# Finishing a decoder layer's output rows beside the longest of 32 experts, run last

## The chip, the cores and the metric

One Trainium2 chip, one of its cores. The metric is device time in microseconds (us) of one launch of the whole layer, the median of several runs.

## What is computed

A decoder layer on 1024 tokens of 1024 features, in f32: a mixer (dilated attention beside a gated linear recurrence), then a mixture of experts. Only the second half matters here:

```python
x = x + gate_m * rms_norm(mixer(...), g_post_mix)          # called x1 below
h = modulate(rms_norm(x, g_pre_ffn), shift_f, scale_f)
top_val, top_idx = lax.top_k(h @ w_router + b_router, 4)   # 4 of 32 experts for each token
gates = softmax(top_val)
# for each chosen expert e of a token:
hg = h @ w_gu[e] + b_gu[e]                                  # 1024 x 2048
act = min(glu, 7) * sigmoid(1.702 * min(glu, 7)) * (clip(lin, -7, 7) + 1)
y += gate * (act @ w_down[e] + b_down[e])                   # 1024 x 1024
x = x + gate_f * rms_norm(y, g_post_ffn)                    # the output
```

An output row needs its token's whole sum y, since the norm is over the row.

## The kernel before, in words

The mixer ends with `mix_out_tile` (L1367), eight times for 128 tokens: it makes x1, stores it straight into the output tensor (L1405, queue of SyncE, SP), stores the rows h of the experts in `hrows` (L1416), and routes. `y_init` (L225) writes to `yacc`, a tensor in HBM, what the down biases give each token; the experts add to it. The experts are sorted by their number of tokens, and rank k gets `CAPS[k]` columns (L26): 352, 288, 256, ... 136 for ranks 0 to 15 (class `Many`), 128 for ranks 16 to 29 (`Few`), 64 for ranks 30 and 31 (`Half`). Tokens beyond the capacity go to a loop at the end, `overflow` (L1503), which has nothing to do on these inputs.

`moe` (L661) runs the ranks in the order `ORDER` (L28): 1, 30, 0, 31, then 2, 16, 3, 17, ... 15, 29. An expert's weights come in 12 pieces of 1 MB, eight for `gu` (the first product and the gating) and four for `down`. SP loads a piece into one of four raw buffers (L307, L313); ScalarE (ACT) copies it to a rounded high part `wh`, and VectorE (DVE) makes the rest `wl` (`split`, L268), four instructions of each. TensorE (PE) multiplies three times, high by high, low by high and high by low. In `Many` the weights stand still and the tokens move (`gemm`, L514), 48 matmuls of n columns' work a piece; with n of 192 to 256, `down` has the tokens stand still and 512 columns of weights move (`down_rows`, L349), 12 matmuls for each block of 128 tokens and piece; larger and smaller `Many` turn the product by PE transposes (L585). `Few` take 12 matmuls of 512 columns a piece, `Half` 8. The product is scaled by the gate on its way out of PSUM, and POOL (GpSimd) adds the rows to `yacc` with an indirect accumulating DMA (`scatter`, L624), one expert's after the other's. The next expert's first quarter of `gu` stands between the current one's `gu` and `down`. `Side` (L635) holds work cut into steps, transposes above all, and after each piece runs up to two steps of what is due; the tile framework then orders the instructions of each engine by priority in the order they were written, and each engine runs its own in order. POOL's queue is in order too: an expert's table and gathers stand behind the last one's additions.

Behind the last expert comes `overflow`, then `final_load` (L1421: the post-norm weights times gate_f, and the loading of the Sqrt table) and `final` (L1432): eight tiles of `yacc` loaded by SP, squared with a row sum on ScalarE, a scale factor from five small VectorE operations and a Sqrt, one product, and an accumulating store on POOL's queue, which adds the tile to x1 in the output (L1456).

Of the kernel before, what the change touches and what calls it, by code (L numbers as in the profile page):

```python
# [27 lines left out]
ORDER = [1, 30, 0, 31] + [k for i in range(2, 16) for k in (i, 14 + i)]  # L28
# [64 lines left out]
def moe_setup(g, tc, cst, wk, dram):  # L93
# [3 lines left out]
    g.yacc = dram.tile([T + TRASH, D], F32, name="yacc")  # L97
    z = wk.tile([128, D], F32, name="zrow", tag="pj")
    nc.vector.memset(z, 0.0)
    nc.gpsimd.dma_start(g.hrows[T:T + TRASH, :], z)  # L100
    nc.gpsimd.dma_start(g.yacc[T:T + TRASH, :], z)
    n = E * TROW // 128
# [15 lines left out]
    g.scats, g.x1st = [], []  # L118
# [366 lines left out]
class Many(Expert):  # L485
# [45 lines left out]
    def gu(self, c, side):  # L531
# [20 lines left out]
        nc.scalar.activation(sg, gl[:, :, 0], AF.Sigmoid, scale=1.702)  # L552
# [40 lines left out]

def get_table(b):
# [5 lines left out]
    b.tab = g.cst.tile([128, 3, 2], I32, name="tab", bufs=3)  # L600
# [60 lines left out]
def moe(g, tc, wp, wk, sm, ps):  # L661
    g.pieces, g.gathered = 0, None
    todo = [(Many if CAPS[k] > 128 else Few if CAPS[k] > 64 else Half)(g, tc, k, (wp, wk, sm, ps)) for k in ORDER]
# [8 lines left out]
    for nxt in todo[1:] + [None]:  # L672
        if nxt:
            prep = nxt.prep()
            side.add(prep)
        side.add(cur.gu(1, side))
# [12 lines left out]
    side.until(last)  # L689
    g.last_y = cur.y[0]  # L690
# [21 lines left out]
def rstd_sqrt(nc, sm, out, ssq, n, shape, name, bufs=None):  # L712

    kw = {} if bufs is None else {"bufs": bufs}
    v = sm.tile(shape, F32, name=name, **kw)
    z = sm.tile(shape, F32, name=name + "z", **kw)
# [7 lines left out]
    return root  # L724

# [637 lines left out]
def mix_out_tile(g, tc, t, wk, sm, ps):  # L1363
# [31 lines left out]
    for hf, cs in enumerate(halves):  # L1395
# [8 lines left out]
        nc.scalar.activation(hT[:, 4 * hf:4 * hf + 4, :].rearrange("p a b -> p (a b)"), pt, AF.Copy)  # L1404
    g.x1st.append(nc.sync.dma_start(g.out[0, tsl, :], x).ins)  # L1405
# [15 lines left out]
def final_load(g, tc, wk, sm):  # L1421
    nc = tc.nc
    g.gf = wk.tile([128, D], F32, name="gf", tag="gl")
    t0 = wk.tile([128, D], F32, name="gf2", tag="gl")
    nc.sync.dma_start(g.gf, g.g_post_ffn.to_broadcast([128, D]))
    nc.sync.dma_start(t0, g.mod_d[5:6, :].to_broadcast([128, D]))
    nc.vector.tensor_mul(g.gf, g.gf, t0)
    one = sm.tile([128, 1], F32, name="f_one")
    nc.scalar.activation(one, g.last_y[:, 0:1], AF.Sqrt, scale=0.0)


def final(g, tc, wp, wk, sm):  # L1432

    nc = tc.nc
    for t in range(0, NT, 2):
        ys = []
        sq = sm.tile([128, 2], F32, name="f_sq", bufs=2)
        for a in range(2):
# [132 lines left out]
def layer(ctx: ExitStack, tc: tile.TileContext, args):  # L1571
# [49 lines left out]
    sm = ctx.enter_context(tc.tile_pool(name="sm2", bufs=1))  # L1621
    moe(g, tc, wp, wk, sm, ps)
    overflow(g, tc, wp, wk, sm, ps)
    final_load(g, tc, wk, sm)
    final(g, tc, wp, wk, sm)


# [20 lines left out]
```

## Time and profile before

| | us |
|---|---|
| three runs: median (lowest to highest) | 2341.78 (2330.75 to 2345.35) |
| the profiled execution: time | 2336.89 |
| its span, first to last instruction | 2335.3 |
| PE busy | 2204.5 (94%) |
| VectorE busy | 1754.9 (75%) |
| ScalarE busy | 1439.3 (62%) |
| POOL busy | 287.5 (12%) |

The profile is of one execution. Busy PE time is a sum over pipelined matmuls whose ends are modelled, so it isn't work at peak rate. An engine counts as idle while it issues DMAs or waits. A number such as L1456 is the line of the kernel before.

### The profile page before, as it was taken

The numbers are of one execution on the slowest core, as the hardware profiler recorded it, in microseconds if no ns is written. First come the engines' busy times: TensorE is split into PE (matmuls) and PEld (weight loads), VectorE is DVE, ScalarE is ACT, GpSimd is POOL, SyncE is SP. The second block draws the span as 40 slices with busy tenths as digits, with TensorE's granted clock in tenths as the row PEclk, the third lists the DMA queues.
The fourth block names the chain that finished last, engine by engine and source line by source line (L and its number), as shares of the span: only waits on it lengthen the run. The fifth ranks groups of instructions, "written<-read, shape, count | busy, mean of one in ns | idle before, by whom it ended". The sixth has DMA issues, their size and how long they took to land. (4 is left out here: it accounts for less than half of the span.)

```text
span 2335.3 us, 38804 instructions
## 1 busy us (share of the span) xinstructions
PE 2204.5 (94%) x13342; PEld 1869.2 (80%) x13342; DVE 1754.9 (75%) x3881; ACT 1439.3 (62%) x3094; POOL 287.5 (12%) x244
## 2 busy tenths in 40 slices
PE   6999999998986999999999999999999999999991
PEld 3766667886766999888788888979999899889881
DVE  6466547556775675878787787978889899889883
ACT  6343442333445674876676676767777777777772
POOL 1000000000233020201110111101201111111101
PEclk9999999998987999999999999999999999999995
DMA  7333201113337695989888898989999999999996
GB/s 264 109 100 106 77 19 51 37 46 115 127 136 239 222 281 180 291 261 300 255 287 276 270 304 261 319 263 304 313 285 320 311 293 317 307 303 322 312 298 154
DMA packets 399217, 527.62 MB, mean 226 GB/s; under 512 B 17204, under 2 KB 308332, under 8 KB 397928
## 3 DMA queue, kind: packets, MB, share of 16 engines
q1 hardware_dynamic: 381296, 471.93, 61.1%
q0 software_dynamic: 16384, 48.54, 9.1%
q10 hardware_dynamic: 1336, 4.63, 0.5%
q8 instruction: 106, 1.74, 0.3%
q14 instruction: 95, 0.78, 0.1%
HBM read 485.29 MB, written 39.75 MB: 225 GB/s over the span
## 5 line engine op out<-in xcount | busy, mean ns | idle before, releaser
L281 DVE TENSOR_TENSOR wl<-raw,wh 128x512 fp32r<-128x512 f32 x1536 | 974.0, 683 | 149.7 <-ACT wh L280 59.5
L280 ACT ACTIVATE wh<-raw 128x512 fp32r<-128x512 f32 x1536 | 852.5, 624 | 242.9 <-DMA raw<-in_w_down_dram 65.6
L528 PE MATMUL pgb<-xb,wh 128*128 128x288 f32 (+13 forms) x2304 | 472.7, 332 | 4.4 <-DVE gl L548 3.9
L528 PEld LDWEIGHTS pgb<-xb,wh 128*128 128x128 f32 x2304 | 360.2, 190 | 13.3 <-DVE gl L548 4.9
L528 PE MATMUL pgb<-xb,wl 128*128 128x288 f32 (+15 forms) x2048 | 301.1, 274 | 0.0
L528 PEld LDWEIGHTS pgb<-xb,wl 128*128 128x128 f32 x2048 | 290.3, 190 | 5.3 <-DVE wl L281 0.2
L625 POOL DMA_INDIRECT yacc<-y,tab x52 | 114.7, 2206 | 1031.7 <-ACT y L369 488.9
L288 PE MATMUL pg<-wh,xh 128*128 128x512 f32 x448 | 180.8, 404 | 0.0
L289 PE MATMUL pg<-wh,xl 128*128 128x512 f32 x448 | 175.8, 392 | 0.0
L528 PE MATMUL pdb<-ab,wh 128*128 128x288 f32 (+7 forms) x768 | 142.5, 314 | 0.0
L988 PE MATMUL pp<-hh,pwh 128*128 128x512 f32 x448 | 130.4, 411 | 8.0 <-DVE y L1048 4.4
L546 ACT ACTIVATE gl<-pgb,bcol 128x288 f32<-128x288 f32 (+15 forms) x256 | 94.1, 421 | 70.8 <-PE pgb L528 70.5
L988 PE MATMUL pp<-hl,pwh 128*128 128x512 f32 x448 | 130.6, 408 | 0.8 <-DVE hl L925 0.8
L988 PE MATMUL pp<-hh,pwl 128*128 128x512 f32 x448 | 129.1, 406 | 0.0
L291 PE MATMUL pg<-wl,xh 128*128 128x512 f32 x448 | 120.8, 392 | 0.0
L528 PEld LDWEIGHTS pdb<-ab,wh 128*128 128x128 f32 x768 | 115.1, 189 | 1.0
L988 PEld LDWEIGHTS pp<-hh,pwh 128*128 128x128 f32 x448 | 82.3, 193 | 26.4 <-DVE y L1048 4.8
L291 PEld LDWEIGHTS pg<-wl,xh 128*128 128x128 f32 x448 | 84.7, 189 | 18.3
L288 PEld LDWEIGHTS pg<-wh,xh 128*128 128x128 f32 x448 | 84.4, 188 | 16.9
L289 PEld LDWEIGHTS pg<-wh,xl 128*128 128x128 f32 x448 | 84.6, 189 | 15.9
L988 PEld LDWEIGHTS pp<-hh,pwl 128*128 128x128 f32 x448 | 81.5, 190 | 19.6 <-issue 5.4
L365 PE MATMUL pd<-wh,ab 128*128 128x512 f32 (+5 forms) x384 | 96.8, 394 | 0.0
(446 smaller groups left out, 3416.9 us busy)
## 6 DMA issues: line engine op xcount, KB each, us to landing
raw<-in_w_gu_dram SPq DMA_DIRECT2D x512, 512.0 KB, 4.9
raw<-in_w_down_dram SPq DMA_DIRECT2D x128, 1024.0 KB, 6.6
wada<-in_w_ada_dram SPq DMA_DIRECT2D x32, 512.0 KB, 3.8
wraw<-in_w_in_dram SPq DMA_DIRECT2D x28, 512.0 KB, 4.0
wada<-in_w_ada_dram SPq DMA_DIRECT2D x8, 1024.0 KB, 8.7
x<-in_x_dram SPq DMA_DIRECT2D x8, 512.0 KB, 3.6
oraw<-in_w_out_dram SPq DMA_DIRECT2D x8, 512.0 KB, 4.2
xo<-in_x_dram SPq DMA_DIRECT2D x8, 512.0 KB
```

The lines of the kernel that those rows point to most:

```text
L280: nc.scalar.activation(h, r, AF.Copy)
L281: nc.vector.tensor_sub(lo, r, h.bitcast(F32))
L288: nc.tensor.matmul(out, xh[:, k0 + i, :], wh[:, i, :], start=start and i == 0, stop=False)
L289: nc.tensor.matmul(out, xl[:, k0 + i, :], wh[:, i, :], start=False, stop=False)
L291: nc.tensor.matmul(out, xh[:, k0 + i, :], wl[:, i, :], start=False, stop=stop and i == HK - 1)
L365: nc.tensor.matmul(p[j][:r], m(j, a, s * HK + i), w[:, i, :], start=s + a + i == 0 and w is wh, stop=s == 1 and w is wl and i == HK - 1)
L528: nc.tensor.matmul(o, w, x, start=s == 0 and j == 0, stop=s == 1 and j == len(seq) - 1, skip_group_check=True)
L546: nc.scalar.activation(gl[:, t, h], src, AF.Identity, bias=self.bias[:, j:j + 1])
L625: b.tc.nc.gpsimd.indirect_dma_start(out=b.g.yacc[:, :], out_offset=bass.IndirectOffsetOnAxis(ap=rows, axis=0), in_=y, in_offset=None, comp ...
L988: nc.tensor.matmul(p, a[:, kt, :], b[:, kt, hs], start=n == 0, stop=n == 3 * KT - 1)
```

## The change

The order of the experts is a new one, with rank 0 (352 columns) last, as a class `Last`. x1 is stored a second time, to a tensor `x1` of its own. While the last expert runs, `final_rows` makes the output rows of all tokens from the sums as they were before it, in steps on the side, with loads on POOL's queue, a scale factor without Sqrt (`rstd_steps`, 13 small VectorE operations for two tiles) and the same accumulating stores. `Last.begin` gathers the last expert's own tokens' rows of x1 and yacc, six indirect loads. Its `down` takes first both column halves of the first half of K, then the second half column half by column half, with tokens standing still in all three blocks. It adds the product to the gathered sums as it leaves PSUM, sums squares half by half, and `close` writes each block's output rows with a plain indirect store, which waits for the eight stores of `final_rows`. The blocks' stores don't wait for one another; the sums go back to yacc behind them, for the overflow loop, which now corrects output rows itself. The diff, shortened:

```diff
-ORDER = [1, 30, 0, 31] + [k for i in range(2, 16) for k in (i, 14 + i)]
+LAST = 0
+ORDER = [2, 16, 15, 17, 1, 30, 18, 3, 31, 14, 19, 4, 20, 13, 21, 5, 22, 12, 23, 6, 24, 11, 25, 7, 26, 10, 27, 8, 28, 9, 29,
+         LAST]
...
+    g.x1 = dram.tile([T + TRASH, D], F32, name="x1")
+    nc.gpsimd.dma_start(g.x1[T:T + TRASH, :], z)
...
         sg = self.wk.tile([128, 2, n], F32, name="sgb", tag="sg")
         nc.vector.tensor_scalar_min(gl[:, :, 0], gl[:, :, 0], 7.0)
-        nc.scalar.activation(sg, gl[:, :, 0], AF.Sigmoid, scale=1.702)
+        self.sigmoid = nc.scalar.activation(sg, gl[:, :, 0], AF.Sigmoid, scale=1.702).ins
...
+class Last(Many):
+    def begin(self, side):
+        nc, g = self.tc.nc, self.g
+        self.pre = final_rows(g, self.tc, self.wk, self.sm)
+        side.add(self.pre, 3)
+        self.rows, self.scats = [], []
+        tags = (("xh", "xl"), ("ah", "al"), ("row", "row"))
+        for (o, r), tag in zip(self.blocks, tags):
+            self.rows.append([self.wk.tile([128, D], F32, name=n, tag=t)[:r] for n, t in zip(("lx", "ly"), tag)])
+        for a, src in enumerate((g.x1, g.yacc)):
+            for j, (o, r) in enumerate(self.blocks):
+                gather(self.tc, self.rows[j][a], src, self.tab[:r, j, 0:1])
+        self.sq = self.sm.tile([128, len(self.blocks), 2], F32, name="l_sq")
+    def down(self, s, side):
+        nc, g = self.tc.nc, self.g
+        nb = len(self.blocks)
+        if s == 0:
+            pp = [self.ps.tile([128, 2, 512], F32, name="pdl", tag="mm") for _ in range(nb)]
+            self.p = [[pp[n // 2][:, n % 2] for n in range(c * nb, c * nb + nb)] for c in range(2)]
+        for c in range(2):
+            cs = slice(c * 512, (c + 1) * 512)
+            wh, wl = self.piece(load_dn, c, s)
+            if c == 1 and s == 1:
+                side.until(self.pre)
+                self.out = [self.wk.tile([128, D], F32, name="lo", tag="row")[:r] for o, r in self.blocks]
+            for j, (o, r) in enumerate(self.blocks):
+                p = self.p[c][j][:r]
+                for a, w in ((0, wh), (1, wh), (0, wl)):
+                    for i in range(HK):
+                        nc.tensor.matmul(p, self.a[:, s * HK + i, a, o:o + r], w[:, i, :],
+                                         start=s + a + i == 0 and w is wh, stop=s == 1 and w is wl and i == HK - 1)
+                if s == 1:
+                    y = self.rows[j][1][:, cs]
+                    nc.vector.scalar_tensor_tensor(y, p, self.tab[:r, j, 1:2].bitcast(F32), y, op0=OP.mult, op1=OP.add)
+                    nc.scalar.activation(g.junk[:r, cs], y, AF.Square, accum_out=self.sq[:r, j, c:c + 1])
+                    if c == 1:
+                        self.close(j, r)
+            side()
+    def gu(self, c, side):
+        super().gu(c, side)
+        if c == 3:
+            with self.tc.issue_after(self.sigmoid):
+                self.tc.nc.scalar.preload_act_table_set("sqrt_and_others")
+    def close(self, j, r):
+        nc, g = self.tc.nc, self.g
+        x, y = self.rows[j]
+        v = self.sm.tile([128, 1], F32, name="l_v", bufs=2)
+        nc.vector.tensor_add(v[:r], self.sq[:r, j, 0:1], self.sq[:r, j, 1:2])
+        self.scats.append(put_rows(g, self.tc, self.sm, self.tab[:r, j, 0:1], x, y, v, self.out[j]))
+        if j == len(self.blocks) - 1:
+            last = self.scats[-1]
+            for i, (x, y) in enumerate(self.rows):
+                self.scats.append(nc.gpsimd.indirect_dma_start(
+                    out=g.yacc[:, :], out_offset=bass.IndirectOffsetOnAxis(ap=self.tab[:y.shape[0], i, 0:1], axis=0),
+                    in_=y, in_offset=None, bounds_check=T - 1, oob_is_err=False).ins)
+                self.tc.add_manual_dep(self.scats[-1], last.name, NOSYNC, reason="the output comes first")
+            for n, a in enumerate(self.scats):
+                for b in self.scats[:n]:
+                    self.tc.declare_no_dep(a, b, reason="an expert's pairs have different tokens")
+def put_rows(g, tc, sm, tok, x, y, ssq, o):
+    nc = tc.nc
+    r = o.shape[0]
+    f = sm.tile([128, 1], F32, name="l_r", bufs=2)
+    nc.vector.tensor_mul(o, y, g.gf[:r])
+    rstd_sqrt(nc, sm, f[:r], ssq[:r], D, [128, 1], "l_p", bufs=2, rows=r)
+    nc.vector.scalar_tensor_tensor(o, o, f[:r], x, op0=OP.mult, op1=OP.add)
+    st = nc.gpsimd.indirect_dma_start(out=g.out[0], out_offset=bass.IndirectOffsetOnAxis(ap=tok, axis=0),
+                                      in_=o, in_offset=None, bounds_check=T - 1, oob_is_err=False)
+    for s in g.outs:
+        tc.add_manual_dep(st.ins, s.name, SYNC, reason="the rows as they were before")
+    return st.ins
+def gather(tc, dst, src, rows):
+    tc.nc.gpsimd.indirect_dma_start(out=dst, out_offset=None, in_=src[:, :],
+                                    in_offset=bass.IndirectOffsetOnAxis(ap=rows, axis=0))
-    b.tab = g.cst.tile([128, 3, 2], I32, name="tab", bufs=3)
+    b.tab = g.cst.tile([128, 3, 2], I32, name="tab", bufs=4)
...
 def moe(g, tc, wp, wk, sm, ps):
-    todo = [(Many if CAPS[k] > 128 else Few if CAPS[k] > 64 else Half)(g, tc, k, (wp, wk, sm, ps)) for k in ORDER]
+    todo = [(Last if k == LAST else Many if CAPS[k] > 128 else Few if CAPS[k] > 64 else Half)(g, tc, k, (wp, wk, sm, ps))
+            for k in ORDER]
...
             prep = nxt.prep()
+        else:
+            final_load(g, tc, wk)
+            cur.begin(side)
...
-    side.until(last)
-    g.last_y = cur.y[0]
...
+def rstd_steps(nc, sm, out, ssq, n, shape, name):
+    v = sm.tile(shape, F32, name=name + "v", bufs=2)
+    z = sm.tile(shape, F32, name=name + "z", bufs=2)
+    nc.vector.tensor_scalar(v, ssq, 1.0 / n, EPS, op0=OP.mult, op1=OP.add)
+    nc.vector.tensor_scalar(z.bitcast(I32), v.bitcast(I32), 1, None, op0=OP.arith_shift_right)
+    nc.vector.tensor_scalar(out.bitcast(I32), z.bitcast(I32), -1.0, float(0x5F3759DF), op0=OP.mult, op1=OP.add)
+    nc.vector.tensor_scalar_mul(v, v, -0.5)
+    for _ in range(3):
+        nc.vector.tensor_mul(z, out, out)
+        nc.vector.tensor_mul(z, z, v)
+        nc.vector.scalar_tensor_tensor(out, z, 1.5, out, op0=OP.add, op1=OP.mult)
...
+    nc.sync.dma_start(g.x1[tsl, :], x)
...
-def final_load(g, tc, wk, sm):
-    nc = tc.nc
-    g.gf = wk.tile([128, D], F32, name="gf", tag="gl")
-    t0 = wk.tile([128, D], F32, name="gf2", tag="gl")
-    nc.sync.dma_start(g.gf, g.g_post_ffn.to_broadcast([128, D]))
-    nc.sync.dma_start(t0, g.mod_d[5:6, :].to_broadcast([128, D]))
-    nc.vector.tensor_mul(g.gf, g.gf, t0)
-    one = sm.tile([128, 1], F32, name="f_one")
-    nc.scalar.activation(one, g.last_y[:, 0:1], AF.Sqrt, scale=0.0)
-def final(g, tc, wp, wk, sm):
-    nc = tc.nc
+def final_load(g, tc, wk):
+    nc = tc.nc
+    t = wk.tile([128, 2, D], F32, name="gf", tag="bgs", bufs=1)
+    nc.sync.dma_start(t[:, 0], g.g_post_ffn.to_broadcast([128, D]))
+    nc.sync.dma_start(t[:, 1], g.mod_d[5:6, :].to_broadcast([128, D]))
+    g.gf = t[:, 0]
+    nc.vector.tensor_mul(g.gf, g.gf, t[:, 1])
+    g.junk = wk.tile([128, D], BF, name="junk", tag="junk", bufs=1)
+def final_rows(g, tc, wk, sm):
+    nc = tc.nc
+    def load(t):
+        ys = [wk.tile([128, D], F32, name="fy", tag="row") for _ in range(2)]
+        for a, y in enumerate(ys):
+            nc.gpsimd.dma_start(y, g.yacc[(t + a) * 128:(t + a + 1) * 128, :])
+        return ys
+    todo = [load(0), load(2)]
+    yield
     for t in range(0, NT, 2):
-        ys = []
+        ys = todo.pop(0)
-        for a in range(2):
-            y = wp.tile([128, D], F32, name="fy", tag=("raw", "wh", "raw", "wl")[(t + a) % 4])
-            nc.sync.dma_start(y, g.yacc[(t + a) * 128:(t + a + 1) * 128, :])
-            jk = wk.tile([128, D], F32, name="fj", tag="row")
-            nc.scalar.activation(jk, y, AF.Square, accum_out=sq[:, a:a + 1])
-            ys.append(y)
+        for a, y in enumerate(ys):
+            nc.scalar.activation(g.junk, y, AF.Square, accum_out=sq[:, a:a + 1])
+        yield
-        z = sm.tile([128, 2], F32, name="f_z", bufs=2)
-        v = sm.tile([128, 2], F32, name="f_v", bufs=2)
-        nc.vector.tensor_scalar(v, sq, 1.0 / D, EPS, op0=OP.mult, op1=OP.add)
-        nc.scalar.activation(z, v, AF.Sqrt)
-        nc.vector.reciprocal(r, z)
-        nc.vector.tensor_mul(z, r, r)
-        nc.vector.tensor_mul(z, z, v)
-        nc.vector.tensor_scalar(z, z, -0.5, 1.5, op0=OP.mult, op1=OP.add)
-        nc.vector.tensor_mul(r, r, z)
+        rstd_steps(nc, sm, r, sq, D, [128, 2], "f_")
+        yield
             st = nc.gpsimd.dma_start(g.out[0, (t + a) * 128:(t + a + 1) * 128, :], y, accum_op=OP.add)
             tc.add_manual_dep(st.ins, g.x1st[t + a].name, SYNC, reason="the sum's other part")
+            g.outs.append(st.ins)
+            yield
+        if t + 4 < NT:
+            todo.append(load(t + 4))
...
+        tok = tab[:, 0, 0:1]
         nc.gpsimd.indirect_dma_start(
-            out=g.yacc[:, :], out_offset=bass.IndirectOffsetOnAxis(ap=tab[:, 0, 0:1], axis=0),
+            out=g.yacc[:, :], out_offset=bass.IndirectOffsetOnAxis(ap=tok, axis=0),
             in_=y, in_offset=None, compute_op=OP.add)
+        x1 = wk.tile([128, D], F32, name="x1v", tag="row")
+        gather(tc, x1, g.x1, tok)
+        ya = wk.tile([128, D], F32, name="yav", tag="row")
+        gather(tc, ya, g.yacc, tok)
+        sq = sm.tile([128, 1], F32, name="v_sq")
+        nc.scalar.activation(g.junk, ya, AF.Square, accum_out=sq)
+        put_rows(g, tc, sm, tok, x1, ya, sq, wk.tile([128, D], F32, name="lov", tag="row"))
...
-    final_load(g, tc, wk, sm)
-    final(g, tc, wp, wk, sm)

```

## Rows read from the trace of the kernel before

**Rows 1.** The page: the span, and its 40 slices of 58.4 us.

```profile
span 2335.3 us, 38804 instructions
...
PE   6999999998986999999999999999999999999991
...
DMA  7333201113337695989888898989999999999996
```

**Rows 2.** Windows: us, busy PE, PEld, DVE, ACT, POOL (instructions), clock, DMA share, GB/s.

```profile
750.00:1000.00 250.00, 250.00 (x1575) 229.76 (x1574) 178.46 (x320) 169.38 (x330) 32.96 (x23) 1.00 0.79 247
750.00:2200.00 1450.00, 1442.32 (x8661) 1289.82 (x8660) 1209.88 (x2280) 1052.05 (x2132) 195.80 (x135) 1.00 0.90 286
2000.00:2200.00 200.00, 197.55 (x1301) 179.12 (x1300) 179.12 (x357) 153.44 (x323) 27.99 (x21) 1.00 0.97 309
2200.00:2287.00 87.00, 82.09 (x521) 73.44 (x519) 73.44 (x141) 63.31 (x130) 7.03 (x3) 0.98 0.85 273
```

**Rows 3.** Waits of PE, longest first, 750:2250 and then 2250:2287.

```profile
PE pgb L528 <- DVE gl L548: 3.9, 5, 1.1
...
PE pts L299 <- DVE act L327: 3.1, 2, 2.9
```

**Rows 4.** The end in order of time: start, us, what, idle before.

```profile
2285.67 1.07 PE L365 MATMUL pd<-wl,ah 128*128 128x512 f32 x4
2286.78 0.69 ACT L369 ACTIVATE y<-pd,tab 128x512 f32<-128x512 f32 x1 [3.02 <-PE pd L365]
2287.74 1.59 POOL L625 DMA_INDIRECT yacc<-y,tab  x1 [16.53 <-ACT y L369]
2294.80 3.90 SPq L1440 DMA_DIRECT2D fy<-yacc  x8
...
2318.33 0.86 POOL L1456 DMA_DIRECT2D out_dram<-fy  x1 [0.34 <-DVE fy L1455]
```

**Rows 5.** POOL's DMAs by line: ns min/median/max; landings of L1456.

```profile
L1456 POOL DMA_DIRECT2D out_dram<-fy x8: 844/882/1194, 2307.4 to 2318.3; - x8
...
DMA to landing us min/median/max: 5.4/8.7/12.4
...
L625 POOL DMA_INDIRECT yacc<-y,tab x52: 1325/1754/6932, 816.3 to 2287.7; - x52
...
L616 POOL DMA_INDIRECT xg<-hrows,tab x50: 865/1198/7440, 713.4 to 2190.5; - x50
```

**Rows 6.** Groups of instructions after 2285: count, busy us, mean ns, idle before.

```profile
L1455 DVE SCALAR_TENSOR_TENSOR fy<-fy,f_r,gf 128x1024 f32<-128x1024 f32 x8 | 9.9, 1282 | 0.1
...
L1448 ACT ACTIVATE f_z<-f_v 128x2 f32<-128x2 f32 x4 | 0.7, 199 | 2.0 <-DVE f_v L1447 2.0
...
L1452 DVE TENSOR_SCALAR f_z<-f_z 128x2 f32<-128x2 f32 x4 | 0.7, 168 | 0.1
```

**Rows 7.** PE in order of time, in ranks 0 and 27.

```profile
868.10 1.54 PE L528 MATMUL pgb<-xb,wh 128*128 128x352 f32 x8
...
875.25 1.45 PE L528 MATMUL pgb<-xb,wl 128*128 128x352 f32 x8
...
2104.93 1.17 PE L365 MATMUL pd<-wh,ah 128*128 128x512 f32 x4
...
2115.90 0.69 PE L528 MATMUL pgb<-xb,wh 128*128 128x288 f32 x4
```

**Rows 8.** DMA issues: count, KB each, median us to landing.

```profile
raw<-in_w_down_dram SPq DMA_DIRECT2D x128, 1024.0 KB, 6.6
...
fy<-yacc SPq DMA_DIRECT2D x8, 512.0 KB, 8.7
...
yacc<-zrow POOLq DMA_DIRECT2D x1, 512.0 KB, 3.9
```

**Rows 9.** POOL, the bias load that each Many issues once: ranks 14, 15.

```profile
2046.26 0.57 POOL L496 DMA_DIRECT2D br<-in_b_gu_dram  x1
...
2133.95 0.55 POOL L496 DMA_DIRECT2D br<-in_b_gu_dram  x1
```

More of the change, by code (lines that the diff above doesn't have):

```diff
@@ L117, in moe_setup @@
     nc.vector.memset(g.Msb, 0.0)
-    g.scats, g.x1st = [], []
+    g.scats, g.outs, g.x1st = [], [], []
 def moe_biases(g, tc, wp, wk):
@@ L709, in rstd, with rstd_sqrt @@
     return ln, ex
-def rstd_sqrt(nc, sm, out, ssq, n, shape, name, bufs=None):
+def rstd_sqrt(nc, sm, out, ssq, n, shape, name, bufs=None, rows=128):
     kw = {} if bufs is None else {"bufs": bufs}
-    v = sm.tile(shape, F32, name=name, **kw)
-    z = sm.tile(shape, F32, name=name + "z", **kw)
+    v = sm.tile(shape, F32, name=name, **kw)[:rows]
+    z = sm.tile(shape, F32, name=name + "z", **kw)[:rows]
     nc.vector.tensor_scalar(v, ssq, 1.0 / n, EPS, op0=OP.mult, op1=OP.add)
@@ L1509, in overflow @@
         rg = nc.gpsimd.value_load(g.lst[0:1, 1, ds(i, 1)], min_val=0, max_val=E * TROW - 128)
-        tab = g.cst.tile([128, 3, 2], I32, name="tab", bufs=3)
+        tab = g.cst.tile([128, 3, 2], I32, name="tab", bufs=4)
         nc.gpsimd.dma_start(tab[:, 0, :], g.table[ds(rg, 128), :])
```

## The prediction, made before the change ran

> **What bounds the kernel now.** I read the page first, then windows over the experts' stage, then who waited for whom on PE, then the end in order of time. The page shows a span of 2335.3 us with PE at nine tenths or more from slice 14 on, and a last slice in which PE does next to nothing while the DMA engines are busy [rows 1]. The windows say the same with numbers: from 750 to 2200 us PE is busy all but some 8 us, while from the first to the last part of it the DMA share climbs from 0.79 to 0.97 and VectorE (DVE) from 178 of 250 to 179 of 200 us [rows 2]. Busy matmuls can hide waits, so I checked who waited: PE's longest total for one cause is 3.9 us in those 1500 us, and it waited 3.1 us at the end of the last expert [rows 3]. So the experts' stage is bound by PE's own instructions. Their number and shapes hardly change with the order of the experts; **a new order can win little there, and can lose**. DMA and VectorE are close behind PE in the second half.
>
> The end is different. The last matmul group ends at 2285.67 + 1.07 = 2286.7; from there to 2335.3 there are 48.5 us without PE [rows 4]: the last product is evicted and added to the sums in HBM (first load of the sums at 2294.8), eight tiles of sums are loaded, squared and scaled, and eight accumulating stores go out. The last store is issued at 2318.33 and lands up to 12.4 us later [rows 4, 5], at 2330.7; 4.6 us of program end follow. Stores landing 8.7 us after issue at the median, and 12.4 for the last, show a queue of transfers rather than a slow engine. These 48.5 us are what the change attacks.
>
> **Part 1, the tail.** Let E be the end of the last matmul. What must still come behind E for the last of three row blocks: one product half evicted (0.69 us, as the 128x512 eviction), its Square over half the columns (0.7 by the same row, and a small read of the sum like the Sqrt), an add of 0.17, a 128x1024 product (1.28, the mean of the eight old ones), five more operations of 0.17 and a Sqrt of 0.20, and the last 128x1024 combination of 1.28; with small gaps 5.8 us [rows 4, 6]. VectorE's share of a block is 4.4 us, but PE finishes a block every 12 x 0.2285 = 2.7 us (forty-eight such matmuls took 2104.93 to 2115.90 [rows 7]), so the three blocks queue: the first is done 5.5 us before E, and 3 x 4.4 us later is E + 7.8; if VectorE also idles for ScalarE in each block it is E + 11.7. I take E + 9. Then POOL issues the last block's output rows and three writes of the sums. No row shows these plain indirect writes beside little else: an accumulating one took 1.59 at the end, a gather 0.865 at best [rows 4, 5]. I take 1.6 + 0.3 for each (bounds 1.2 and 7.2 with the gap); the fourth is issued at E + 9 + 3 x 1.9 = E + 14.7 and lands 3.9 us after issue, as the plain 512 KB write from POOL to the same tensor did [rows 8]: E + 18.6. The loop that finds no overflow lies in the 7.1 us from 2287.74 to 2294.80 [rows 4], of which the landing of the last additions takes some 6; I put it at 0.85, an estimate. The program end is 4.6: E + 24. **48.5 becomes 24, a gain of 24.5** (30 with the short ends, 18 where the stores of the first pass hold the output rows up, below).
>
> **Part 2, what moves under the last expert.** Eight loads of sums, six gathers and eight accumulating stores go to POOL's queue, with the squares, the scale factors and the products. On VectorE that is 8 x 1.28 + 4 x 13 x 0.17 = 19 us, on ScalarE by the eviction's rate 8 x 2 x 0.69 = 11 us, on POOL 16 x 0.9 + 6 x 1.2 = 22 us, and on the DMA engines the twenty or so us that the eight stores took when alone (2307.4 to 2330.7, one each 2.5 us once they queue [rows 4, 5]). The cover is the longest expert: 44 of its matmuls ran from 868.10 to 875.25, 0.1625 us each, so the 48 of a piece of weights take 7.8 us of PE, while a Few piece takes 2.7 [rows 7]. Twelve pieces are 94 us of PE. In the stretch that held this expert VectorE was idle 72 of 250 us [rows 2], 27 in 94; ScalarE and POOL had more. There is room. If the cover fails, the price is that work laid behind E, at most the old tail. Waiting instructions can still stand in front of the splits on their engine, so I add 2 us (0 to 15). The last down product by rows is 144 matmuls of 0.2285 = 32.9 us; before it was 192 of 0.1625 = 31.2 and 24 output transposes of 128 columns, by their columns some 2 us: 0.
>
> **Part 3, the drain.** In the last 87 us before E PE is busy 82.1 [rows 2], since the last expert was a small one whose final pieces are short for PE. Behind expert 0 the pieces are already there: a gain of 4 (0 to 5).
>
> **Part 4, the order.** Supply of weights: the last pairs of experts take 2133.95 - 2046.26 = 87.7 us at a DMA share of 0.97 [rows 2, 9], 3.65 us for each of 24 pieces. PE takes 2.74 us for the 12 matmuls of a Few piece, and for the 8 of a Half piece, of the same 512 columns, 1.83 [rows 7]. PE's stock is at most four raw and three split pieces, 25 us of supply, of which the landing of a 1 MB piece (6.6 us [rows 8]) and the splitting behind it use about half: 12 to 16 us can be run down. Before, a Half stood between the two largest and never ran down more than 6 x (3.65 - 1.83) = 11 us; PE indeed did not wait there [rows 2, 3]. Now 30 is followed by 18: six Half pieces, two Few, four Half, six Few run 11 + 1.8 + 7.2 + 5.5 = 25 us down before expert 3 gives back; with the supply at 3.3 us a piece, if little else is moved, it is 19. That leaves 3 to 13 us of waiting. A second, weaker place is 31, 14, 19 (1 to 5). Elsewhere a large expert, a Few, a middle one and a Few come to more PE time than supply. I take +6 (-5, were the 7 us of waits in the second half to go, to +18).
>
> **Part 5, small parts.** Eight more 512 KB stores of x1 through SP in the output projection: the DMA share was 0.4 or less there by the page's slices 10 to 12 [rows 1]; PE, not SP, sets that stage: 0 (to +2, before the first expert's rows can be gathered). The Sqrt table is loaded ahead under the matmuls; in the old tail it came behind the loads, and is gone with Part 1. Fourth table buffer, zero rows of x1: 0.
>
> **Sum.** -24.5 - 4 + 6 + 2 = -20.5 us against the profiled execution's 2336.89 (span 2335.3 and 1.6 around it): 2316.4. The runs' median, 2341.78, is 4.9 above; I forecast between the two bases, **2318 us**, own range 2307 to 2329.
>
> **A rule against it.** POOL's indirect writes of rows took 1325 ns at best, 1754 at the median and up to 6932; its gathers 865, 1198 and 7440; its plain stores in the empty tail 844 to 1194 [rows 5]. So beside busy engines most are a third slower, and a few are six times as long. The Trainium skill, "SBUF — State Buffer", section "SBUF: two separate sides", says that POOL cannot write its descriptors while certain VectorE operations hold a shared port, and gives 620 ns growing to 3100. By that factor of five, an estimate from that page, each of the closing writes would take about 5 us. The trace agrees for the few long rows and not for the median, and I keep the median.
>
> **Rivals.**
> *A, the stock of weights runs dry (slower).* If only one piece (4 us) could be run down, each of fourteen Few would lack 43.8 - 36 - 4 = 3.8 us and each Half 43.8 - 24 - 4 = 15.8: 53 + 32 = 85 us of waits in place of 6, 2397. It decides from 27 us of waits on. For it: DMA and VectorE are at 97 and 90% late. Against: the pairs of a large and a Few expert, in which every Few lacks 7.8 us, ran with PE busy throughout [rows 2, 3].
> *B, the first pass is late.* Tiles 4 to 7 reuse buffers, so their loads wait for stores to land (8.7), and the next loads take 8.7 again [rows 5, 8]. If the last pair is squared only in the final 8 us, its stores land at E + 9 to E + 12, and only then may the first output rows go: E + 12, five more issues of 1.9, 3.9 and 5.4 is E + 31: 2325; with 10 us more of lateness, 2335. For it: the steps are bound to pieces. Against: VectorE and ScalarE run several pieces ahead of PE.
> *C, POOL is held up at the end.* If three of the six closing writes take the 6.9 us of the longest row in place of 1.6, the tail is 16 us longer: 2334. By the Trainium skill's figure above, an estimate, all six would take 5 us: +20, 2338. It holds where VectorE's last products lie beside POOL's issues.
> *D, no loss from the order and a tight tail.* Tail 30, drain 5, order -3: 2336.9 - 38 + 4 (the median's side) = 2303.
>
> **Chances.** Forecast 0.45, D 0.2, B 0.19, C 0.08, A 0.08. A measurement of this kernel tells about 1% (23.4 us) from no change, so the line is at 2318.4: half the forecast, a little more, and D lie below it: faster 0.48. Half the forecast, B and C lie within: same 0.44. A and the ends of B and C: slower 0.08. The range for 8 in 10 cuts the far part of A and the best of D: 2292 to 2346.
>
> **What would show it.** Right: behind the last matmul some 24 us, with no load of sums in it, and POOL's last six indirect writes ending it; PE waits of 3 to 13 us at the experts 30 and 18, few at the end; the eight accumulating stores landed before E. Wrong: output rows waiting on those stores (B); POOL's writes of over 3 us in the tail (C); PE idle many times over the whole experts' stage, with the clock falling (A); or PE's total busy time changed by more than some 10 us, which would break the premise that the order leaves PE's work alone.

## The result: slower, and the profile after

The changed kernel takes 2355.22 us (median of 7 runs, 2351.18 to 2359.29) against 2334.31 for the kernel before in runs beside it: a ratio of 1.0076 [1.0061, 1.0091]. The profiled execution took 2355.61 us, its span 2353.9. It is 0.8% slower, with an interval clear of 1. The forecast of 2318 and the range of 2292 to 2346 missed it, on the slow side.

The tail did shrink, but the last matmul came much later. In order of time, the end of the changed kernel (its own line numbers here and below: L633 is the last product, L1564 the accumulating store, L674 the last step of the output rows on VectorE, L675 their writing, L658 the writing of the sums):

```profile
2323.04 1.09 PE L633 MATMUL pdl<-wl,ab 128*96 128x512 f32 x4
...
2326.93 0.85 POOL L1564 DMA_DIRECT2D out_dram<-fy  x1 [43.34 <-DVE fy L1563]
2328.12 0.85 POOL L1564 DMA_DIRECT2D out_dram<-fy  x1 [0.35 <-DVE l_r L818]
...
2333.34 1.28 DVE L674 SCALAR_TENSOR_TENSOR lo<-lo,l_r,lx 96x1024 f32<-96x1024 f32 x1
2336.25 1.05 POOL L675 DMA_INDIRECT out_dram<-lo,tab  x1 [7.28 <-DMA out_dram<-fy]
...
2342.74 0.93 POOL L658 DMA_INDIRECT yacc<-ly,tab  x1 [0.30 <-issue]
```

E, the end of the last matmul, is 2324.1, against 2286.7 [rows 4]: 37.4 us later. The tail is 2353.9 - 2324.1 = 29.8 us, against 48.5: 18.7 less. What is left is the 18.7 us by which the profiled execution is slower. POOL's 7.28 us of idling stand for two accumulating stores of the first pass that were issued behind E and had to land before an output row could go: rival B.

Where the 37.4 us came from, by windows (columns as in [rows 2]):

```profile
750.00:1000.00 250.00, 246.92 (x1571) 223.80 (x1571) 200.10 (x373) 173.97 (x352) 27.06 (x19) 1.00 0.85 273
1000.00:1250.00 250.00, 235.13 (x1323) 196.29 (x1322) 204.33 (x393) 182.42 (x371) 43.51 (x27) 0.97 0.91 291
...
2000.00:2200.00 200.00, 200.00 (x1245) 183.29 (x1244) 177.36 (x339) 152.19 (x315) 31.22 (x21) 1.00 0.95 303
2200.00:2300.00 100.00, 88.16 (x480) 83.26 (x479) 65.10 (x131) 50.04 (x93) 20.27 (x21) 0.93 0.81 239
```

PE lost 15 us in the second stretch (247.95 busy before) and 12 in the last, and the clock is below 1.00 in just these two. In each stretch between them it is as busy as it was, to 0.2 us, or busier. The last stretch has one cause, by the waits of PE from 2200 to 2300:

```profile
PE pgb L532 <- ACT gl L550: 11.8, 2, 8.0
```

gl is the eviction of the gating product from PSUM, on ScalarE. ScalarE wasn't busy then; it stood waiting, with the evictions queued behind:

```profile
2245.58 1.06 ACT L1557 ACTIVATE junk<-fy 128x1024 bf16<-128x1024 f32 x1 [10.72 <-DMA fy<-yacc]
...
2248.19 0.97 ACT L550 ACTIVATE gl<-pgb,bcol 128x352 f32<-128x352 f32 x2
...
2272.39 1.06 ACT L1557 ACTIVATE junk<-fy 128x1024 bf16<-128x1024 f32 x1 [5.45 <-DMA fy<-yacc]
...
2273.45 1.87 ACT L550 ACTIVATE gl<-pgb,bcol 128x352 f32<-128x352 f32 x4
```

Squares of the first pass (L1557) wait for their loads of sums (L1548), and the loads wait on POOL:

```profile
2240.97 2.21 POOL L1548 DMA_DIRECT2D fy<-yacc  x4 [8.11 <-DMA yacc<-y,tab]
...
2264.80 0.55 POOL L1548 DMA_DIRECT2D fy<-yacc  x1 [4.91 <-DMA out_dram<-fy]
```

The two waits have different reasons. The first loads wait for the expert before to be added to the sums (8.11 us from 2232.9 to 2241.0). The later one, behind PE's longer wait of 8.0 us, fills a buffer of the first pass that is free only when the pass's own store from it has landed. In the second stretch the waits have many names. The longest, at expert 18 behind the Half expert 30, in order of time:

```profile
1043.68 2.19 ACT L284 ACTIVATE wh<-raw 128x512 fp32r<-128x512 f32 x4 [4.53 <-DMA raw<-in_w_gu_dram]
1045.78 0.36 ACT L305 ACTIVATE ah<-pts 128x256 fp32r<-128x256 f32 x1
...
1046.17 0.42 DVE L306 TENSOR_TENSOR al<-pts,ah 128x256 fp32r<-128x256 f32 x1 [3.90 <-ACT ah L305]
...
1046.65 0.32 PE L507 MATMUL pxb<-ident,xg 112*128 112x112 f32 x1 [3.21 <-DVE al L306]
```

The row of PE names VectorE, VectorE names ScalarE, and ScalarE names a piece of weights that hadn't landed: the stock was gone. And such a wait can be paid for twice: here the clock of the next 7 us is 0.76 of full speed:

```profile
1048.00:1055.00 7.00, 7.00 (x27) 5.55 (x26) 5.23 (x11) 4.42 (x10) 2.08 (x3) 0.76 0.90 263
```

To add waits and half clock up I use one measure for all kernels: the **excess**, the sum over PE's matmuls from 728 us on of the time from one's start to the next's, less the median of that time for the same three neighbours (line and shape) over all 14 traces. For the change, E moves by 24.2 (728 to 1300 us) - 2.4 (1300 to 2200) + 11.2 (2200 to E) + 4.4 (the medians themselves, of which 2.1 is the later start of the experts, 724.7 against 722.6): 37.4.

| kernel | median us | ratio to before [95%] | E | tail | excess to 1300 | to 2200 | to E |
|---|---|---|---|---|---|---|---|
| before | 2334.31 | 1 | 2286.7 | 48.5 | 6.1 | 9.7 | 7.2 |
| changed | 2355.22 | 1.0076 [1.0061, 1.0091] | 2324.1 | 29.8 | 30.3 | 7.3 | 18.4 |
| order_alone | 2381.92 | 1.0190 [1.0161, 1.0219] | 2316.0 | 62.7 | 35.1 | 8.5 | 1.1 |
| order_back | 2342.92 | 1.0021 [1.0004, 1.0037] | 2315.7 | 29.5 | 11.2 | 21.0 | 18.9 |
| behind | 2348.89 | 1.0054 [1.0035, 1.0074] | 2315.4 | 29.5 | 30.7 | 8.2 | 11.2 |
| early_end | 2346.81 | 1.0049 [1.0032, 1.0066] | 2321.4 | 21.4 | 28.1 | 7.7 | 17.5 |
| forced | 2338.72 | 1.0014 [0.9996, 1.0032] | 2304.7 | 29.3 | 27.7 | 7.2 | 1.7 |
| mended | 2363.35 | 1.0119 [1.0081, 1.0157] | 2324.2 | 29.5 | 13.7 | 28.7 | 16.2 |
| no_pass | 2328.60 | 0.9959 [0.9942, 0.9976] | 2307.2 | 20.6 | 28.6 | 10.1 | 1.4 |
| best | 2344.96 | 1.0029 [1.0009, 1.0050] | 2309.0 | 21.4 | 11.0 | 22.4 | 10.2 |
| few_first | 2328.18 | 0.9956 [0.9939, 0.9973] | 2302.2 | 30.9 | 14.7 | 16.9 | 1.8 |
| forced_xb | 2338.12 | 1.0005 [0.9989, 1.0021] | 2311.2 | 21.4 | 29.0 | 6.2 | 9.1 |
| all3 | 2328.16 | 0.9961 [0.9946, 0.9976] | 2300.9 | 21.4 | 14.8 | 9.1 | 9.3 |
| all4 | 2321.36 | 0.9944 [0.9922, 0.9966] | 2297.1 | 21.9 | 13.7 | 14.7 | 1.0 |

Ratio and median come from all runs, the last five columns from one profiled execution; those of 'best' and 'mended' were 13 and 8 us quicker than their medians, that of 'few_first' 7 us slower. So the columns say where time lies, the ratios how much (0.001 is 2.3 us; the kernel before had medians of 2334 to 2339 beside them).

### The profile page after: what moved, and what is told of

Its sections match the earlier page's. It is cut to its first block, busy times and chain, and to the rows that moved or that the text cites. A ratio compares the mean times of both kernels' runs of the same rounds, so it can differ in the third digit from the quotient of the medians.

```text
span 2353.9 us, 38769 instructions
## 1 busy us (share of the span) xinstructions
PE 2218.8 (94%) x13270; PEld 1868.1 (79%) x13270; DVE 1771.5 (75%) x3942; ACT 1431.0 (61%) x3092; POOL 298.2 (13%) x262
## 5 line engine op out<-in xcount | busy, mean ns | idle before, releaser
L532 PE MATMUL pgb<-xb,wh 128*128 128x352 f32 (+13 forms) x2304 | 476.5, 335 | 15.0 <-ACT gl L550 11.8
L532 PE MATMUL pgb<-xb,wl 128*128 128x256 f32 (+15 forms) x2048 | 303.7, 276 | 2.8 <-DVE wl L285 2.6
L718 POOL DMA_INDIRECT yacc<-y,tab x49 | 125.8, 2568 | 1110.7 <-ACT y L373 587.2
L550 ACT ACTIVATE gl<-pgb,bcol 128x256 f32<-128x256 f32 (+15 forms) x256 | 93.1, 422 | 64.8 <-PE pgb L532 64.3
L532 PE MATMUL pdb<-ab,wh 128*128 128x288 f32 (+7 forms) x640 | 121.2, 316 | 4.3 <-DVE yt L580 4.3
L532 PEld LDWEIGHTS pdb<-ab,wh 128*128 128x128 f32 x640 | 95.5, 192 | 5.9 <-DVE yt L580 5.1
L293 PEld LDWEIGHTS pg<-wh,xl 128*128 128x128 f32 x448 | 84.8, 189 | 15.9
```

The costliest lines, as they stand in the source:

```text
L293: nc.tensor.matmul(out, xl[:, k0 + i, :], wh[:, i, :], start=False, stop=False)
L532: nc.tensor.matmul(o, w, x, start=s == 0 and j == 0, stop=s == 1 and j == len(seq) - 1, skip_group_check=True)
L550: nc.scalar.activation(gl[:, t, h], src, AF.Identity, bias=self.bias[:, j:j + 1])
L718: b.tc.nc.gpsimd.indirect_dma_start(out=b.g.yacc[:, :], out_offset=bass.IndirectOffsetOnAxis(ap=rows, axis=0), in_=y, in_offset=None, comp ...
```

## The experiments

Theory: three separate causes, the order (some 20 us), squares in front of evictions (some 15) and the last pair of the first pass (8). Rivals: the new traffic itself, or something else in the new end.

**Run order_alone.** The kernel before with the changed order and no more:

```diff
-ORDER = [1, 30, 0, 31] + [k for i in range(2, 16) for k in (i, 14 + i)]
+ORDER = [2, 16, 15, 17, 1, 30, 18, 3, 31, 14, 19, 4, ... 8, 28, 9, 29, 0]
```

> The kernel before with the changed order of experts and nothing else; expert 0 ends it in the old form, with the old last pass behind it. Theory 'order': the six Half pieces of expert 30 followed by the Few expert 18 use up the weights that are ready, PE waits and its clock falls to half, so PE excess time between 1000 and 1250 us is about 20 us, as in the changed kernel (23), against 2 before. A few us come back at the end, as pieces wait for PE behind the longest expert: 2345 to 2355. Rival 'added traffic' (the second copy of x1 and what follows from it cost the time, not the order): no waits there, and the time is within 5 us of the kernel before, or 4 under it for the drain.

Excess 35.1 to 1300 us against 6.1: the order alone brings the waits, without a byte of new traffic. The time is far above the expectation, 2381.92, as I had left out what the old end costs behind expert 0: three additions to the sums that wait for one another, 62.7 us of tail. The waits of PE between 1000 and 1250 us:

```profile
PE pxb L504 <- DMA xg<-hrows,tab: 7.8, 2, 5.6
PE pds L440 <- DVE as L435: 3.7, 1, 3.7
```

Here the longest, at the same place, is for the rows of the next expert (xg), which stand on POOL's queue behind the last one's additions; in the changed kernel it was for weights. A Half expert is too short for both supplies. Which of them binds in a given execution stays open.

**Run order_back.** The changed kernel with the pairs of before, 0 last:

```diff
+ORDER = [1, 30, 2, 31] + [k for i in range(3, 16) for k in (i, 13 + i)] + [29, LAST]
```

> The changed kernel with the order of before (a Half or Few behind each larger expert), expert 0 still last. Theory 'order': the waits between 1000 and 1250 us fall from 23 to under 5 us, and the time from 2355 to about 2335 (2331 to 2340); the 17 us of waits under the last expert and the tail of 30 us stay. Rival 'added traffic': 2350 to 2357.

The waits between 1000 and 1250 us are gone, and 0.0055 (13 us) of the time, less than the 20 expected: with 0 taken out, 31 follows 2 (7.4 us of excess between 900 and 1000), and 28 and 29, two small ones, end the row (10.4 between 2100 and 2200). The rival falls.

**Run behind.** The first pass's steps written behind the evictions, six steps of `final_rows` a call:

```diff
     def gu(self, c, side):
         super().gu(c, side)
+        if c > 1:
+            self.first_pass(6)
...
```

> The changed kernel with the steps of the first pass put behind the evictions of chunks 2 and 3 of the last expert, in place of in front of them; its last pair is as late as it was. Theory 'squares block evictions': PE's waits on gl under the last expert (11.8 us over three, with 13 us at half clock around them) are gone, the excess between 2200 and 2300 us falls from 17 to under 4, the last matmul ends 13 to 17 us earlier and the time is 2338 to 2343, the tail of 30 us unchanged. Rival 'shared bandwidth' (the extra loads, gathers and stores take the DMA engines from the weights): waits on weights in place of those on gl, and no more than 5 us come back.

Only 5 us came back, and the intervals overlap. The order of instructions that the scheduler made has the squares written behind the evictions of chunk 2 in front of those of chunk 1 all the same; why, no run shows. ScalarE again idled 10.93 us, and PE waited for gl again (6.2 us), not for weights. This run didn't test the theory.

**Run early_end.** `side.until(self.pre)` one half of K earlier:

```diff
+            if c == 1 and s == 0:
+                side.until(self.pre)
             if c == 1 and s == 1:
-                side.until(self.pre)
```

> The changed kernel with the rest of the first pass finished one half earlier (ahead of the second piece of the last down product's first half). Theory 'late last pair' (case B of the prediction): the last two accumulating stores are issued 20 us or more before the last matmul ends, the output rows go as soon as each is made, and the tail falls from 30 to 22 to 24 us: 2347 to 2350. Rival 'POOL and the landing set the tail': the six closing writes and the end take as long as before wherever the stores lie; tail 28 to 30, time within 2 us of the changed kernel. A second risk: the squares now wait in front of the splits of the last pieces, and PE waits some us more before the tail.

Tail 21.4, time lower by 0.0027 (6 us): rival B's wait was the changed kernel's. Before the output rows POOL now waits for VectorE alone, and its six writes take 1 us each:

```profile
2322.03 1.05 POOL L676 DMA_INDIRECT out_dram<-lo,tab  x1 [31.58 <-DVE l_pz L817]
...
2327.96 0.94 POOL L676 DMA_INDIRECT out_dram<-lo,tab  x1 [1.54 <-DVE lo L675]
2329.20 0.98 POOL L659 DMA_INDIRECT yacc<-ly,tab  x1 [0.30 <-issue]
```

**Run forced.** As 'behind', with an order on ScalarE that the scheduler must keep:

```diff
+            q = nc.scalar.activation(g.junk, y, AF.Square, accum_out=sq[:, a:a + 1]).ins
+            tc.add_manual_dep(q, g.evict.name, NOSYNC, reason="the gating comes first")
```

> The kernel of run 'behind' with an order that the scheduler must keep on ScalarE: the squares of the first pass stand behind the gl evictions of chunk 2 or 3 of the last expert. (In 'behind' they were written there, and still ran in front of the evictions of chunk 1 and 2, waiting 10.9 and 3.4 us for their loads.) Theory 'squares block evictions': the excess of PE between 2200 and 2300 us falls from 17 (9.6 in 'behind') to under 3, no wait of PE on gl is over 1 us there, the last matmul ends some 15 us earlier than in the changed kernel; tail still 29 to 30, as the last pair is as late as it was; 2336 to 2343. Rival 'shared bandwidth': waits of PE of 5 us or more on wh or wl under the last expert in place of those on gl; 2346 or more.

As expected: no wait of PE on gl, excess from 2200 us 1.7, tail 29.3, time 2338.72, 0.0062 (14 us) off the changed kernel's ratio. Only E moved by more than the 15 us expected, 19.4, of which the excess from 2200 us gives 16.7. ScalarE now waits for PE, not PE for it, with the same loads in place:

```profile
2254.27 1.00 ACT L550 ACTIVATE gl<-pgb,bcol 128x352 f32<-128x352 f32 x2 [2.87 <-PE pgb L532]
2255.16 1.06 ACT L1563 ACTIVATE junk<-fy 128x1024 bf16<-128x1024 f32 x1
```

**Run mended.** A third order, from a sum of PE time against supply:

> The changed kernel with a third order: expert 0 last, the Half experts 30 and 31 and the Few experts each next to larger ones (15, 27, 13, 25, 6, 30, 4, 17, 9, 23, ... 1, 18, ... 19, 3, 22, 11, 26, 0), so that by PE time against supply no place runs more than about 12 us of ready weights down by much. Theory 'order': the excess between 800 and 1300 us falls from 29 (3 + 2 + 11 + 7 + 6) to under 12, and stays under 8 between 1900 and 2200 us; the time is 2333 to 2343. Rival 'added traffic': 24 us or more of waits wherever the small experts lie, 2350 to 2357.

A miss. The early excess fell from 30.3 to 13.7, but 28.7 came up between 1300 and 2200 us, and the time rose to 2363.35. The two longest waits of PE between 1940 and 2000 us lie at the Few experts 21 and 19, which I had put side by side:

```profile
PE pg L292 <- ACT xh L305: 6.4, 1, 6.4
PE pbb L514 <- DVE xb L511: 2.2, 1, 2.2
```

**Run no_pass.** No `side.add(self.pre, 3)` and no `side.until(self.pre)`:

> The changed kernel with the first pass left out but for its first four loads of sums: no squares, products or accumulating stores of it (the output rows of tokens that aren't the last expert's stay x1); six gathers and the last expert's own rows as they were. It bounds what the first pass costs. Theory: no waits on gl under the last expert (excess under 2 between 2200 and 2300 us), output rows issued as soon as they are made, tail 20 to 22: 2329 to 2335. Rival 'the rest of the new end costs it' (gathers, column halves, the longest expert's place): the last matmul ends within 5 us of the changed kernel's 2324 and the tail is over 27.

The first pass costs the changed kernel 1.0076 - 0.9959 = 0.0117, 27 us; 'forced' has 14 of them back with all transfers in place, so they weren't bandwidth. With the tail of 20.6, 9 more are the last pair; some 4 stay open.

**Run best.** The order of 'mended', forced squares, an early end:

> Three parts at once: the order of 'mended', the forced place of the squares of 'forced', and a first pass in two groups of four tiles (squares, products, four stores, then the next four loads), ended a half earlier as in 'early_end'. If the three causes add up, 2355 - 17 (order) - 15 (evictions) - 8 (tail) = 2315 (2308 to 2324), faster than the kernel before by some 20 us. If they overlap (PE's waits moved to another place when one is gone), 2325 to 2340.

2344.96: not the sum. The order was the bad one of 'mended', and PE waited 7 us for an eviction ly that stood behind the last pair on VectorE.

**Runs few_first and forced_xb.** A fourth order, on top of 'forced'; and in another kernel the last pair's own buffer:

```diff
+ORDER = [16, 1, 30, 2, 17, 3, 31, 4, 18, 15, 19, 5, 20, 14, 21, 6, 22, 13, ... 11, 27, 9, 28, 10, 29, LAST]
```
```diff
...
+        if t == 6:
+            v = wk.tile([128, KT, 2, CAPS[LAST]], F32, name="fx", tag="xb").rearrange("p a b c -> p (a b c)")
...
```

> The kernel of run 'forced' with a fourth order, in which no two experts of 128 columns or fewer stand next to each other: 16, 1, 30, 2, 17, 3, 31, 4, 18, 15, 19, 5, 20, 14, 21, ... 28, 10, 29, 0. As the first one now has 128 columns, its biases are loaded before its first quarter. Run 'mended' had two such neighbours late (21, 19) and waited 11 us there. Theory 'neighbours': the excess of PE between 800 and 1300 us falls from 26 (in 'forced') to under 10 and that between 1300 and 2200 us stays under 12; 2317 to 2328. Rival 'the supply is short as a whole': the waits go to other places, the sum from 750 to 2300 us stays at 30 or more, and the time at 2333 or more.

> The kernel of run 'forced', its first pass ended a half earlier as in 'early_end', with the last pair of sums loaded into the space of the last expert's input columns (free after its last gu chunk) in place of buffers that wait for a store to land. (In 'best' the last pair was still late, and an eviction stood behind its squares on VectorE: PE waited 7 us.) Theory: tail 21 to 22, no such wait, the last matmul ends at 2303 to 2307 as in 'forced': 2329 to 2333. Rival: the wait of 'best' (5 us or more on ly) comes again, and the gain of the tail is given back: 2335 or more.

few_first: excess to 1300 us 14.7, of which some 11 from 800 us on (under 10 expected), ratio 0.0058 (14 us) under that of 'forced', the first version that makes all the output rows and is faster than the kernel before. Its excess of 16.9 to 2200 us is mostly one wait near 1584 us with half clock behind it, which 'all3', with the same order, doesn't have. So in this execution the sum from 750 us on is the rival's (30 or more), though the time isn't. forced_xb: the rival's wait on ly came (4.8 us), and with it most of the tail's gain went.

**Runs all3 and all4.** Both together; then one line more:

> Both: the order of 'few_first' and the last pair of 'forced_xb'. If the three causes (order, evictions, last pair) add up, it is 2308 to 2320, faster than the kernel before by 15 to 28 us. If the supply is short as a whole, 2325 to 2335.

> The kernel of run 'all3' with one line changed: each block of the last down product has a PSUM tile of its own for its two column halves, in place of two neighbouring blocks in one tile. In 'all3' PE waited 5.0 us (and ran 6.8 us at half clock behind it) before the second block of the first half, for VectorE's eviction ly of the first block, which stood behind the last pair's scale and products on VectorE. Theory 'shared tile': no wait on ly over 1 us is left, the excess between 2200 and 2300 us falls from 9 to under 2, the tail stays 21 to 22: 2317 to 2323. Rival: PE waits as long for another thing (the wh and wl of the last pieces, whose splits stand behind the same instructions), 2326 to 2330.

all3 gave 2328.16, no better than 'few_first' and inside the range of 'short supply': the tail lost 9.5 us, and PE waited in their place, but not for weights. Its longest wait from 2200 us, and VectorE at that time:

```profile
PE pdl L634 <- DVE ly L638: 5.0, 1, 5.0
```
```profile
2276.39 0.17 DVE L833 TENSOR_SCALAR f_v<-f_sq 128x2 f32<-128x2 f32 x1 [3.58 <-ACT junk L1568]
...
2280.72 2.48 DVE L1575 SCALAR_TENSOR_TENSOR fx<-fx,f_r,gf 128x1024 f32<-128x1024 f32 x2
2283.12 0.75 DVE L638 SCALAR_TENSOR_TENSOR ly<-pdl,tab,ly 128x512 f32<-128x512 f32 x1
```

PE didn't need what ly makes, only the other half of the PSUM tile that ly reads. all4 gives each block a tile:

```diff
-            self.p = [[pp[n // 2][:, n % 2] for n in range(c * nb, c * nb + nb)] for c in range(2)]
+            self.p = [[pp[n][:, c] for n in range(nb)] for c in range(2)]
```

```profile
PE pdl L634 <- DVE ly L638: 0.8, 1, 0.8
```

The wait is 0.8 us, the time 2321.36 and the ratio 0.9944 [0.9922, 0.9966]: faster than both kernels, by 13 us and by 31 (0.0132). The interval overlaps that of all3, so what the line itself gave, some 4 us, rests on the wait that is gone and not on the times.

## Why the prediction was wrong, point by point

By the prediction's own steps, for the profiled executions (E and tail as above):

| step | forecast us | came out |
|---|---|---|
| Part 1, tail | -24.5 | -18.7 |
| Part 2, under the last expert | +2 (0 to 15) | +18.4 |
| Part 3, drain | -4 | -7.2 |
| Part 4, order | +6 (-5 to +18) | +24.2 early, -2.4 late |
| Part 5, small | 0 (to +2) | +2.1 |
| the medians, not assigned | | +2.3 |
| sum | -20.5 | +18.7 |

The last product's own time was forecast rightly: 33.7 us from 2288.9 to 2324.1 without its one wait, against 31.0 and 2.4 of transposes before. The 2.1 of Part 5 is not shown to be a cost of the second x1: six kernels with the same code up to there begin their experts anywhere from 721.6 to 725.4 us.

**What bounds the kernel: right.** PE does, and that the order "can win little there, and can lose" is what it did. PE's total busy time rose by 14.3 us (2204.5 to 2218.8), over the 10 that the prediction named as a sign against its premise. Some 8 of these are the clock and not other work, an estimate: among the experts PE was busy for 23.2 us at half clock, against 6.7 before, and half of the difference is lost.

**Part 2 failed most.** I weighed busy time against room, 11 us on ScalarE beside 94 of PE, and there was room. The step that fell is "Waiting instructions can still stand in front of the splits on their engine, so I add 2 us". They stood in front of the evictions, which have no stock behind them as splits have: there are three PSUM tiles and a chunk (two pieces of `gu`) takes two, so PE stops a quarter of a chunk later (24 matmuls, 3.9 us). I had the number: an accumulating store lands 8.7 us after its issue at the median [rows 5], and here the first load waited 8 us for the last addition, a later one 4.9 us for a store of the pass itself. Rival B named that second wait, but priced it in the tail alone. 'forced' shows the cause, since the same work in another order costs 1.7.

**Part 4: place right, size wrong.** The waits came where the prediction put them, at 30 and 18 and then at 31, 14 and 19, and PE idled 13 us more there between 1000 and 1250 us, inside the 4 to 18 that the working gave; the whole term, 21.8, came out above its bound of 18. I had taken +6, near the low end, and left out two things. Some of the waits were followed by half clock (13.6 us of it in that stretch, some 7 us lost), and the first experts (15 beside 16 and 17, excess 3.3 between 800 and 900) had a place of their own. Rival A needed 27 us of waits. PE idled 15.9 us more from 750 to 1250, so 24 of excess is reached only with the half clock; and A's sign, idling over the whole stage, wasn't there: 2.8 us from 1250 to 2200, against 5.6 before. The stock did run dry, at a few places in place of all.

**Part 1: the choice against rival B was wrong.** I gave B 0.19. Its working said E + 31, and 29.8 came; its condition, a last pair squared only in the final 8 us, held (2315.7, E - 8.4). I had set against it that ScalarE runs pieces ahead of PE. It does, but in its own order: the pair stood behind the first squares of the last product (L638):

```profile
2309.33 0.63 ACT L638 ACTIVATE junk<-ly 128x512 bf16<-128x512 f32 x1 [14.33 <-DVE ly L637]
...
2315.69 1.06 ACT L1557 ACTIVATE junk<-fy 128x1024 bf16<-128x1024 f32 x1
```

So B was right in its tail and not in its reason: the pair's loads, which B had as the late ones, were issued at 2275.3 and 2277.8 and had landed by 2282.5, 33 us before. Without that wait the tail is 21.4 (early_end), 2.6 under my 24: the third block's rows go at E + 6.6 (I took 9), POOL's writes follow each other at 1.3 us, not 1.9, and from the last issue to the end it is 11.0, not 9.4.

**Rival C didn't come.** The closing writes took 0.93 to 1.05 us each, below the shortest accumulating one, 1.33 [rows 5]. In the changed kernel its condition wasn't there: VectorE's last product ended at 2334.6, and the first write went at 2336.3. In 'early_end' the first two writes lay beside VectorE for 1.16 and 0.79 us and took 1.05 and 1.01. The factor of five that the Trainium skill gives ("SBUF — State Buffer", section "SBUF: two separate sides") for descriptors blocked by VectorE didn't show in the closing writes of any run. Elsewhere in the changed kernel indirect issues did take long beside VectorE, when it made its splits (wl) one directly behind the other:

```profile
1190.55 9.43 POOL L718 DMA_INDIRECT yacc<-y,tab  x1 [20.24 <-ACT y L483]
```
```profile
1187.66 10.93 DVE L285 TENSOR_TENSOR wl<-raw,wh 128x512 fp32r<-128x512 f32 x18
```

This longest one ended 1.4 us behind the last of 18 splits. From 700 us on 15 indirect issues took over 3 us, and 13 of them ended 1.4 to 1.6 us behind such a row of splits; not every issue that began in a row was held (1.59 us at 1047.0). So the long rows on which C built are real, but what VectorE does at the end didn't bring them; no run took the splits away.

**The chances.** B came true in its tail and A at a few places, beside a Part 2 beyond its bounds. I had weighed the causes as if at most one went wrong, and three did. Two of them, the evictions and the last pair, are alike: on ScalarE, an instruction whose data had come stood behind one that still waited. By the prediction's own line of 1% (23.4 us) the 20.9 us between the medians are "same", which had 0.44; but they lie on the slow side, and the forecast was on the fast one.

## What to carry to other kernels

When work is moved beside the bounding engine, ask of every instruction that waits for memory which eviction stands behind it on its engine, and read that from the order the scheduler made, not from the code; an order-only dependency can be worth as much as the whole idea (14 us here). Jobs that use up weights faster than they come should have no neighbour of their kind. Where a change has a gain and several costs, take its parts alone: the idea here was good for 13 us once its side effects (order, evictions, last pair, shared tile) had been found one by one and taken away or made smaller.

## What the runs showed of the hardware that I hadn't expected

Short waits of PE can cost more than themselves, by the granted clock. In the changed kernel 3.2 us of waiting, ended at 1046.7, were followed by 3.4 us at half (1.2 GHz) from 1048.4; the 8.0 us that ended at 2274.5 had 10.2 us at half around their end; in 'all3' 5.0 us had 6.8. A wait of 1.5 us at 1231 was followed by 6.8 us at half, one of 1.6 at 1416 in 'all4' by none.

A wait can be for a neighbour: two PSUM halves that no instruction shares, in one tile, made PE wait 5.0 us, and 0.8 with a tile for each block. PE waits there for a semaphore of VectorE that the program holds; whether the chip itself needs that order, no run shows.

An indirect issue of POOL can last as long as VectorE's splits beside it: 9.43 us in the changed kernel, against 0.89 to 1.75 for the 26 that had no split beside them.
